# A chunked recurrence whose step matrix becomes block-diagonal over two heads, with the scaled state written by ScalarE

## The chip, the cores and the metric

The kernel runs on one core of one Trainium2 chip. The metric is the device time of one execution in microseconds (us). The core's engines are called as in the profile: PE is TensorE's matmul, PEld its weight load, DVE is VectorE, ACT is ScalarE, POOL is GpSimd, SP is SyncE, which issues most transfers. Each engine works through its own queue in order, and an instruction that waits for a semaphore holds what is behind it.

## The reference

The model is one block of width 1024 over a sequence of 1024: attention with a forget gate (8 heads of 64), an RWKV-7 time mix (8 heads of 64), a gated merge, and a feed-forward part with a convolution. All is in fp32. The change lies in the time mix, whose core is a recurrence over time for each head:

```python
def step(state, inp):
    r_t, w_t, k_t, v_t, a_t, b_t = inp
    sa = jnp.einsum('bhvk,bhk->bhv', state, a_t)
    state = state * w_t[:, :, None, :] + sa[..., None] * b_t[:, :, None, :] + v_t[..., None] * k_t[:, :, None, :]
    y_t = jnp.einsum('bhvk,bhk->bhv', state, r_t)
    return state, y_t
```

## The kernel before

The time mix is computed in chunks of 64 positions, so that only one 64x64 state for each head and chunk is handed on. Two heads sit on the 128 partitions together (head 0 on partitions 0 to 63, head 1 on 64 to 127; HS[h] is the slice). The four head pairs p and two halves hf of the sequence (512 positions, 8 chunks) make eight units. A unit has two generators. `pre` builds its inputs: it loads the decay `cum` and `al` (L707, L709), takes the running sum of cum within each chunk (the scan at L710), its exponentials el and en (L713, L715), the products p (L758), a 31-step triangular inverse on VectorE (L778, L780) with round trips through DRAM (sm, M, se, TT), and the transposes vt and at. `main` first completes the inverse (xi, zi, and the copies of TT at L853), then forms uw (Wt, UV), then mz, from which VectorE writes Zt (L877) and the step matrix Mt (L878: product plus identity, both heads of a chunk stacked as 128x64). The recurrence follows: for each chunk c, sp (which already holds the input part) gets Mt times the state S of that chunk added, one 64x64 product for each head, and S of the next chunk is sp times the chunk's decay pcd (L897, VectorE). At the end all states enter yp with Zt (one 64x64 product for each head and chunk), and the output y is normalised: `head_sums` splits its argument in two parts (L688 on ScalarE, L689 on GpSimd) and sums over each head by two matmuls with blk_r, once for mu and once for va. Then the gate gg is loaded (L929), multiplied in, and the result stored.

A unit has 8 state operations in the first half of the sequence and 7 in the second. The first state of a head pair needs no product, so there are 56 steps with products and 60 state operations. Each product is one `mm`; the profile counts two records for an fp32 product, so 224 in all (L141 is the line of the helper through which nearly all matmuls go).

TensorE's order is written out by the class `Weave`: it keeps a model time, runs the chains `main` and `pre` as they come due, and fills the model time that a `yield` asks for with large matmuls (the projections ps_rkv, qk, v and gt, 128x128 weights by 512 or 256 columns). The recurrence yields 1150 after each step, which puts about six of the 512-wide matmuls, or eleven of the 256-wide ones of v, between two steps. `mm_cost` prices a 64x64 fp32 product at half of what it prices a full-size one of the same output. The other engines' orders come from the tile scheduler, which goes by an estimate of when each input is ready; buffers of the same tag are reused, and a new user waits for the readers of the old one. Zt, Mt and Wt are single buffers, which the split parts of `head_sums` (Zt and Mt) and gg (Wt) take over once the recurrence is through.

What else the change and the prediction touch: L366 (ScalarE's scaled copy of a projection), L272 and L274 (the split of large weights in two parts, on ScalarE and VectorE), L393 (ScalarE's write of q and k), L734 (ScalarE's copy of bk), L805 and L866 (copies of at and uw), L742 (VectorE's ksq). The lines that the changed kernel moves have other numbers there (L853 is L859, L688 is L692).

Of the kernel before, what the change touches and what calls it, by code (L numbers as in the profile page):

```python
# [9 lines left out]
F32 = mybir.dt.float32  # L10
F32R = mybir.dt.float32r
AF = mybir.ActivationFunctionType
ALU = mybir.AluOpType
# [3 lines left out]
S = 1024  # L17
KT = 8
NH = 512
# [3 lines left out]
CH = 64  # L23
NCU = NH // CH
# [13 lines left out]
CST = {}  # L38
# [6 lines left out]
NC1 = 384  # L45
NC2 = CST["blk"][0]
# [86 lines left out]
def hybrid_block(ctx: ExitStack, tc: tile.TileContext, a, out):  # L133
    nc = tc.nc
# [3 lines left out]
    def mm(o, lhsT, rhs, start, stop, more=False):  # L138

        weave.mm_cost(o, lhsT, rhs)  # L140
        nc.tensor.matmul(o, lhsT, rhs, start=start, stop=stop, skip_group_check=more)  # L141
# [5 lines left out]
    def f32(ap):  # L147
        return ap.bitcast(F32)

    tt, stt, ts = nc.vector.tensor_tensor, nc.vector.scalar_tensor_tensor, nc.vector.tensor_scalar  # L150
# [11 lines left out]
    cst = cp.tile([128, NC1], F32R, name="cst")  # L162
# [6 lines left out]

    def C(name):  # L170
        o, k = CST[name]
        return cst[:, o : o + k] if o < NC1 else cst2[:, o - NC1 : o - NC1 + k]

    eye_r, tri_r = C("ident"), C("tri")
    ident, ones = f32(eye_r), f32(C("ones"))
# [68 lines left out]
    marks = {}  # L244
# [101 lines left out]
    with ExitStack() as es:  # L346
        scr = es.enter_context(tc.tile_pool(name="scr", bufs=2, space=bass.MemoryType.DRAM))
        shp = es.enter_context(tc.tile_pool(name="shp", bufs=2))
        cst2 = shp.tile([128, NC2 - NC1], F32, name="cst2", bufs=1)

        def big(name):
            return pb.tile([128, NH], F32, tag="big", name=name)
# [48 lines left out]
        HS = (slice(0, 64), slice(64, 128))  # L401
# [11 lines left out]
        with tc.tile_pool(name="st", bufs=1) as st, tc.tile_pool(name="stp", bufs=2, space=PS) as stp, \  # L413
# [113 lines left out]
                for j in range(2):  # L527
                    nc.sync.dma_start(w2[r * 64 : r * 64 + 64, j * 512 : j * 512 + 512], a["w2a2"][j * 64 : j * 64 + 64, :])
            nc.sync.dma_start(g2, a["g2"])
            nc.sync.dma_start(cst2, a["cst"][:, NC1:NC2])  # L530
            for i in (1, 0):
                for kt in range(KT):
                    mod_add(kt, *m[1 - i])
# [23 lines left out]
        with tc.tile_pool(name="lg", bufs=1, reuse_waits="tile") as lg, \  # L557
# [65 lines left out]
            def forget():  # L623

                wf = lg.tile([128, 8, 40], F32R, tag="wf", name="wf", bufs=1)
                wr = lg.tile([128, 8, 8], F32, tag="wr", name="wr", bufs=1)
                nc.sync.dma_start(wr, a["w_f"])
                ts(wf, cst2[:, 0:320].rearrange("p (k x) -> p k x", x=40), 0.0, None, op0=ALU.mult)
                nc.scalar.copy(wf[:, :, 0:8], wr)
                tt(wf[:, :, 32:40], wr, f32(wf[:, :, 0:8]), op=ALU.subtract)  # L630
                bf = lg.tile([8, 1], F32, tag="bf", name="bf", bufs=1)
                nc.sync.dma_start(bf, a["b_f"])
                prev = None
                for hf in range(2):
                    cs = slice(hf * NH, hf * NH + NH)
                    ps = gen(f"f_{hf}")
                    n = 0
                    for x in u:
                        for kt in range(KT):
                            mm(ps[0:40, :], wf[:, kt, :], x[:, kt, cs], start=n == 0, stop=n == 15)  # L640
# [42 lines left out]
        blk_r = rw.tile([128, 128], F32R, name="blk_r")  # L683
        nc.gpsimd.dma_start(blk_r, a["cst"][:, NC2 : NC2 + 128].bitcast(F32R))

        def head_sums(ps, x, hi, lo):

            nc.scalar.copy(hi, x)  # L688
            nc.gpsimd.tensor_tensor(lo, x, f32(hi), op=ALU.subtract)  # L689
            yield 3400  # L690
            mm(ps, blk_r, hi, start=True, stop=False)
            mm(ps, blk_r, lo, start=False, stop=True)  # L692

        def pre(k, p, hf):
# [5 lines left out]
            def tmp(nm, w=NH, bufs=1, dt=F32):  # L700
                return rw.tile([128, w], dt, tag=nm, name=f"{nm}{n}", bufs=bufs)
# [5 lines left out]
            nc.sync.dma_start(cum, d_lora[0, p, :, cs])  # L707
            al = tmp("al")
            nc.sync.dma_start(al, d_lora[1, p, :, cs])  # L709
            nc.vector.tensor_tensor_scan(cum, C("reset"), cum, initial=0.0, op0=ALU.mult, op1=ALU.add)  # L710
            el = chunk_tile("el", 1, NCU, CH + 1)
            nc.gpsimd.memset(el[:, :, 0:1], 1.0)
            nc.scalar.activation(el[:, :, 1:], c3(cum), AF.Exp, scale=-DEC)  # L713
# [37 lines left out]
            for c0 in range(0, NCU, 4):  # L751
                ps = [gen(f"p1_{n}{h}{c0}") for h in range(2)]
                for c in range(c0, c0 + 4):
                    for h in range(2):
                        mm(ps[h][:, (c - c0) * 128 : (c - c0) * 128 + 128], bk[HS[h], c, BKS[h], :], ar[HS[h], :, c, :],
                           start=True, stop=True)
                for h in range(2):
                    marks["E"] = tt(E[:, c0 : c0 + 4, h, 0:2, :].rearrange("p c a s -> p c (a s)"), hx(ps[h], 128),  # L758
                       C("mask").unsqueeze(1).to_broadcast([128, 4, 128]), op=ALU.mult)
                yield 2200  # L760

            sm = scr.tile([2, NCU, 2, 32, 32], F32, tag="sm", name=f"sm{n}")
# [8 lines left out]
            ready = weave.now + (49500 if k == 0 else 38500)  # L771
            E32 = chunk_tile("E32", 1, 8, 32)
            nc.gpsimd.dma_start(E32, a["cst"][:, CST["einit"][0] :].rearrange("p (j t) -> p j t", t=32))
            t32 = tmp("t32", 256)
            for s in range(31):
                J, W = s // 4 + 1, 31 - s
                tv = t32[:, 0 : J * W].rearrange("p (j w) -> p j w", w=W)
# [46 lines left out]
        def main(k, p, hf):  # L824
# [41 lines left out]
                    nc.scalar.copy(UV[HS[h], c0 : c0 + 4, h, :], pv[HS[h], :, 0, :])  # L866
            yield 2970
            Zt = rw.tile([128, NCU, CH], F32, tag="Zt", name=f"Zt{n}", bufs=1)
            Mt = rw.tile([128, NCU, CH], F32, tag="Mt", name=f"Mt{n}", bufs=1)
            for c0 in range(0, NCU, 4):  # L870
                ps = gen(f"mz{n}{c0}")
                for c in range(c0, c0 + 4):
                    for h in range(2):
                        x = (c - c0) * 128
                        mm(ps[HS[h], x : x + 128], Wt[HS[h], c, :], E[HS[h], c, h, 1:3, :], start=True, stop=True)
                pv = ps.rearrange("p (c a s) -> p c a s", a=2, s=CH)
                tt(Zt[:, c0 : c0 + 4, :], pv[:, :, 0, :], ar[:, 1, c0 : c0 + 4, :], op=ALU.add)  # L877
                tt(Mt[:, c0 : c0 + 4, :], pv[:, :, 1, :], C("i2").unsqueeze(1).to_broadcast([128, 4, CH]), op=ALU.add)  # L878

            yp = py.tile([128, NCU, CH], F32, tag="yp", name=f"yp{n}")  # L880
            sp = py.tile([128, NCU, CH], F32, tag="sp", name=f"sp{n}")
# [9 lines left out]
            last_c = NCU - 1 - hf  # L891
            for c in range(last_c + 1):
                if S[c] is not None:
                    for h in range(2):
                        mm(sp[HS[h], c, :], Mt[HS[h], c, :], S[c][HS[h], :], start=False, stop=c == last_c, more=True)
                S.append(rw.tile([128, CH], F32, tag="state", name=f"S{n}{c}", bufs=9))
                marks["S"] = ts(S[-1], sp[:, c, :], pcd[:, c : c + 1], None, op0=ALU.mult)  # L897
                if c + 1 < NCU:
                    yield 1150

# [10 lines left out]
            def part(nm, i):  # L911
                return rw.tile([128, NH], F32R, tag=nm, name=f"{nm}{i}{n}", bufs=1)

            mu = gen(f"mu{n}")
            yield 700
            yield from head_sums(mu, y, part("Zt", "r"), part("Mt", "r"))
            stt(y, mu, -1.0 / CH, y, op0=ALU.mult, op1=ALU.add)
            ysq = rw.tile([128, NH], F32, tag="ysq", name=f"ysq{n}", bufs=1)
            nc.scalar.activation(ysq, y, AF.Square)
            yield 2700  # L920
            va = gen(f"va{n}")
            yield from head_sums(va, ysq, part("Zt", "s"), part("Mt", "s"))
            rs = rw.tile([128, NH], F32, tag="ysq", name=f"rs{n}", bufs=1)
            nc.scalar.activation(rs, va, AF.Ln, scale=1.0 / CH, bias=epsr[:, 1:2])
            nc.scalar.activation(rs, rs, AF.Exp, scale=-0.5)
            stt(y, y, V("ln_w", p), rs, op0=ALU.mult, op1=ALU.mult)
            stt(y, y, V("ln_b", p), bon, op0=ALU.add, op1=ALU.add)
            gg = rw.tile([128, NH], F32, tag="Wt", name=f"gg{n}", bufs=1)
            nc.sync.dma_start(gg, d_lora[2, p, :, cs])  # L929
            ov = rw.tile([128, NH], F32, tag="ysq", name=f"o{n}", bufs=1)  # L930
            tt(ov, y, gg, op=ALU.mult)
# [1078 lines left out]
```

## Time and profile before

| | us |
|---|---|
| time of 3 runs, median (lowest to highest) | 1674.87 (1674.54 to 1675.46) |
| profiled execution, its own time | 1675.02 |
| its span in the trace | 1673.2 |
| PE busy | 1626.0 (97%) |
| PEld busy | 1341.4 (80%) |
| DVE busy | 1224.8 (73%) |
| ACT busy | 804.6 (48%) |
| POOL busy | 130.5 (8%) |

The span is what the trace covers; the execution's own time has 1.8 us more around it. The busy share is an average over the whole block: the projections, the recurrence (about 250 to 640 us), the attention and the feed-forward part have different limits. In rows of the timeline, the first number is the start in us from the span's start, the second the time from the first start to the last end of the group (matmuls overlap, so the starts tell more than the durations); a bracket tells how long the engine was idle before and what ended that. In rows of groups, the columns are the line, engine, operation, out<-in, shapes and count, then busy us and the mean ns of one, then the idle time before them with what ended it. Rows of waits have the total us, how many, and the longest.

### The profile page before, as it was taken

What the parts mean: (1) busy time and instruction counts of PE and PEld (TensorE: products, weight loads), DVE (VectorE), ACT (ScalarE), POOL (GpSimd) and SP (SyncE); (2) the same over time, 40 slices, a digit from 0 to 9 for tenths busy, and PEclk for the clock granted to TensorE, in tenths of its full rate; (3) what the DMA queues carried; (4) which work ended last, traced back from release to release, by engine and by line L of the source; (5) the groups of instructions that cost most, each with busy time, mean ns of one, the idle gap of its engine ahead of it and who ended that gap; (6) DMA issues with size and microseconds to landing.
All of it is one profiled execution on the core that took longest, in us unless ns stands there. A gap on an engine that the chain in (4) does not pass through costs nothing.

```text
span 1673.2 us, 26130 instructions
## 1 busy us (share of the span) xinstructions
PE 1626.0 (97%) x9806; PEld 1341.4 (80%) x9806; DVE 1224.8 (73%) x2407; ACT 804.6 (48%) x1480; POOL 130.5 (8%) x151
## 2 busy tenths in 40 slices
PE   7999999999999999999999999999999999999998
PEld 7777777787877777888878888888888888888886
DVE  5786777788876625898768546897777777786677
ACT  5563334434344456667632225654444444455455
POOL 0011001101111002221022000000000000000000
PEclk9999989999999999999999999999999999999999
DMA  8487644443342227444087511143322323574463
GB/s 334 146 315 239 181 114 124 130 111 112 102 121 76 90 76 181 131 128 120 34 306 267 213 63 64 63 125 109 107 95 96 119 95 108 192 271 154 129 210 108
DMA packets 121502, 240.77 MB, mean 144 GB/s; under 512 B 40032, under 2 KB 48608, under 8 KB 121376
## 3 DMA queue, kind: packets, MB, share of 16 engines
q1 hardware_dynamic: 112896, 220.74, 40.6%
q0 software_dynamic: 8480, 18.37, 4.2%
q8 instruction: 77, 1.26, 0.3%
q14 instruction: 49, 0.40, 0.1%
HBM read 173.51 MB, written 65.54 MB: 143 GB/s over the span
## 4 chain that ended last, share of the span: by engine, by line
PE 74%; DVE 14%; DMA 6%; ACT 3%; issue 2%; SPq 2%; DVEq 0%; ACTq 0%
PE X L141 14%; PE D L141 13%; PE Y L141 7%; PE wo L141 5%; PE ps_rkv L141 5%; PE br L141 5%; PE gt L141 4%; PE rk_ps L141 3%; PE W L141 3%; PE qk L141 2%; PE lg L141 2%; PE ov L141 2%; PE tp L145 2%; DVE E L780 1%; DVE t L778 1%
## 5 line engine op out<-in xcount | busy, mean ns | idle before, releaser
L141 PE MATMUL D<-op,op 128*128 128x512 f32 x924 | 209.8, 389 | 0.0
L141 PEld LDWEIGHTS D<-op,op 128*128 128x128 f32 x924 | 173.3, 188 | 36.3 <-DVE op L1247 0.3
L141 PE MATMUL X<-T_m,S 128*128 128x512 f32 x440 | 106.9, 389 | 0.0
L141 PEld LDWEIGHTS X<-T_m,S 128*128 128x128 f32 x440 | 82.5, 188 | 17.5 <-ACT x L1537 0.4
L1246 ACT CAST op<-g 128x512 fp32r<-128x512 f32 x77 | 47.8, 621 | 74.8 <-PE D L141 47.8
L1247 DVE TENSOR_TENSOR op<-g,op 128x512 fp32r<-128x512 f32 x77 | 53.1, 689 | 41.5 <-ACT op L1246 41.5
L1497 DVE SCALAR_TENSOR_TENSOR c<-ab,vec,c 128x512 f32<-128x512 f32 x88 | 65.9, 750 | 18.4 <-ACT c L1500 16.8
L778 DVE TENSOR_TENSOR t<-E,M 128x60 f32<-128x60 f32 (+24 forms) x248 | 57.0, 230 | 25.9 <-DMA M<-sm 20.4
L1461 DVE TENSOR_TENSOR A<-ur,A 128x512 fp32r<-128x512 f32 x64 | 44.0, 689 | 39.3 <-ACT A L1457 39.1
L1461 DVE TENSOR_TENSOR S<-ur,S 128x512 fp32r<-128x512 f32 x66 | 45.5, 691 | 34.9 <-ACT S L1457 34.8
L274 DVE TENSOR_TENSOR lo_in<-raw_in,hi_in 128x512 fp32r<-128x512 f32 x84 | 57.6, 726 | 14.0 <-PE gt L141 4.6
L1457 ACT CAST S<-ur 128x512 fp32r<-128x512 f32 x66 | 41.0, 622 | 55.6 <-DVE ur L1450 30.6
L141 PE MATMUL Y<-T_h,S 128*128 128x512 f32 x264 | 65.6, 398 | 1.6 <-ACT T_h L1715 1.0
L272 ACT CAST hi_in<-raw_in 128x1024 fp32r<-128x1024 f32 x42 | 43.8, 1047 | 42.5 <-PE ps_rkv L141 25.0
L141 PE MATMUL Y<-T_h,A 128*128 128x512 f32 x264 | 63.4, 389 | 0.0
L1048 ACT ACTIVATE P<-lg,nm 128x896 f32<-128x896 f32 (+3 forms) x64 | 47.4, 743 | 29.1 <-DVE nm L1044 20.9
L141 PEld LDWEIGHTS Y<-T_h,S 128*128 128x128 f32 x264 | 50.6, 192 | 13.4 <-ACT T_h L1715 1.8
L141 PE MATMUL W<-B_f,A 128*128 128x512 f32 x252 | 60.6, 389 | 0.0
L141 PE MATMUL X<-B_b,A 128*128 128x512 f32 x252 | 60.5, 389 | 0.0
L1457 ACT CAST A<-ur 128x512 fp32r<-128x512 f32 x64 | 39.6, 622 | 43.2 <-PE X L141 33.4
L780 DVE TENSOR_TENSOR E<-E,t 128x60 f32<-128x60 f32 (+24 forms) x248 | 55.2, 223 | 5.7
L141 PEld LDWEIGHTS Y<-T_h,A 128*128 128x128 f32 x264 | 49.5, 188 | 10.3
(480 smaller groups left out, 4125.0 us busy)
## 6 DMA issues: line engine op xcount, KB each, us to landing
raw_in<-in_w_in SPq DMA_DIRECT2D x50, 512.0 KB, 3.8
wm<-in_w_mod SPq DMA_DIRECT2D x48, 512.0 KB, 7.3
ur<-in_w_up SPq DMA_DIRECT2D x44, 512.0 KB, 4.0
g<-d_g SPq DMA_DIRECT2D x35, 512.0 KB, 4.0
d_g<-gs SPq DMA_DIRECT2D x44, 256.0 KB, 2.0
d_g<-c SPq DMA_DIRECT2D x33, 256.0 KB, 4.4
d_st<-qh SPq DMA_DIRECT2D x64, 128.0 KB, 2.4
stA<-d_st POOLq DMA_DIRECT2D x8, 1024.0 KB, 6.6
```

The source lines that it names most:

```text
L141: nc.tensor.matmul(o, lhsT, rhs, start=start, stop=stop, skip_group_check=more)
L145: nc.tensor.transpose(o, i, eye)
L272: nc.scalar.copy(hi, raw)
L274: nc.vector.tensor_tensor(lo[:, c : c + NH], raw[:, c : c + NH], f32(hi[:, c : c + NH]), op=ALU.subtract)
L778: tt(tv, E32[:, 0:J, s : s + 1].to_broadcast([128, J, W]), M32[:, s : s + 1, s + 1 : 32].to_broadcast([128, J, W]), op=ALU.mult)
L780: tt(E32[:, 0:J, s + 1 : 32], E32[:, 0:J, s + 1 : 32], tv, op=ALU.add)
L1048: nc.scalar.activation(e[:, 0:n], lg[:, 0:n], AF.Exp, bias=nm[:, 0:1], accum_out=nm[:, 1:2])
L1246: nc.scalar.copy(hi, src)
L1247: tt(lo, src, f32(hi), op=ALU.subtract)
L1457: nc.scalar.copy(hi, src)
L1461: tt(lo, src, f32(hi), op=ALU.subtract)
L1497: stt(c, ab[:, x + hf * NH : x + hf * NH + NH], V("conv_w", 22 * x + i), c, op0=ALU.mult, op1=ALU.add)
```

## The change

- The step matrix Mt is one persistent tile of 128x128 for each chunk, cleared once by GpSimd. VectorE writes the two 64x64 diagonal blocks of each chunk, one instruction for each head and four chunks (32 in all instead of 16 of both heads), adding the block of `ident`.
- A step is one product of 128x128 weights with the 128x64 state of both heads, instead of two of 64x64.
- The next state is written by ScalarE (activation Copy with the scale taken from pcd) instead of VectorE's tensor_scalar. The number of state buffers goes from 9 to 8.
- To make room: the second constant tile keeps 384 of 704 columns (the mask, and 256 columns of `reset`) and is loaded in two transfers; the scan at L710 runs in two halves of 256 columns; t32 shrinks from 256 to 128 columns; the forget weights are cleared from another tile. Since Mt is no longer a free buffer after the recurrence, the split parts of `head_sums` go to Wt, and gg goes to Zt.

```diff
-        cst2 = shp.tile([128, NC2 - NC1], F32, name="cst2", bufs=1)
+        cst2 = shp.tile([128, 384], F32, name="cst2", bufs=1)
...
-            nc.sync.dma_start(cst2, a["cst"][:, NC1:NC2])
+            for o, c0, w in ((0, CST["mask"][0], 128), (128, CST["reset"][0], 256)):
+                nc.sync.dma_start(cst2[:, o : o + w], a["cst"][:, c0 : c0 + w])
...
+        Mt = rw.tile([128, NCU, 128], F32, name="Mt")
+        nc.gpsimd.memset(Mt, 0.0)
...
-            nc.vector.tensor_tensor_scan(cum, C("reset"), cum, initial=0.0, op0=ALU.mult, op1=ALU.add)
+            for c0 in (0, 256):
+                nc.vector.tensor_tensor_scan(cum[:, c0 : c0 + 256], cst2[:, 128:384], cum[:, c0 : c0 + 256], initial=0.0,
+                                             op0=ALU.mult, op1=ALU.add)
...
-                tt(Mt[:, c0 : c0 + 4, :], pv[:, :, 1, :], C("i2").unsqueeze(1).to_broadcast([128, 4, CH]), op=ALU.add)
+                for h in range(2):
+                    tt(Mt[HS[h], c0 : c0 + 4, HS[h]], pv[HS[h], :, 1, :],
+                       ident[HS[h], HS[h]].unsqueeze(1).to_broadcast([64, 4, CH]), op=ALU.add)
...
-                    for h in range(2):
-                        mm(sp[HS[h], c, :], Mt[HS[h], c, :], S[c][HS[h], :], start=False, stop=c == last_c, more=True)
-                S.append(rw.tile([128, CH], F32, tag="state", name=f"S{n}{c}", bufs=9))
-                marks["S"] = ts(S[-1], sp[:, c, :], pcd[:, c : c + 1], None, op0=ALU.mult)
+                    mm(sp[:, c, :], Mt[:, c, :], S[c], start=False, stop=c == last_c, more=True)
+                S.append(rw.tile([128, CH], F32, tag="state", name=f"S{n}{c}", bufs=8))
+                marks["S"] = nc.scalar.activation(S[-1], sp[:, c, :], AF.Copy, scale=pcd[:, c : c + 1])
...
-            yield from head_sums(mu, y, part("Zt", "r"), part("Mt", "r"))
+            yield from head_sums(mu, y, part("Zt", "r"), part("Wt", "r"))
...
-            gg = rw.tile([128, NH], F32, tag="Wt", name=f"gg{n}", bufs=1)
+            gg = rw.tile([128, NH], F32, tag="Zt", name=f"gg{n}", bufs=1)
```

More of the change, by code (lines that the diff above doesn't have):

```diff
@@ L171, in C @@
         o, k = CST[name]
-        return cst[:, o : o + k] if o < NC1 else cst2[:, o - NC1 : o - NC1 + k]
+        return cst[:, o : o + k]
     eye_r, tri_r = C("ident"), C("tri")
@@ L627, in forget @@
                 nc.sync.dma_start(wr, a["w_f"])
-                ts(wf, cst2[:, 0:320].rearrange("p (k x) -> p k x", x=40), 0.0, None, op0=ALU.mult)
+                ts(wf, f32(cst[:, 0:320]).rearrange("p (k x) -> p k x", x=40), 0.0, None, op0=ALU.mult)
                 nc.scalar.copy(wf[:, :, 0:8], wr)
@@ L758, in pre @@
                     marks["E"] = tt(E[:, c0 : c0 + 4, h, 0:2, :].rearrange("p c a s -> p c (a s)"), hx(ps[h], 128),
-                       C("mask").unsqueeze(1).to_broadcast([128, 4, 128]), op=ALU.mult)
+                       cst2[:, 0:128].unsqueeze(1).to_broadcast([128, 4, 128]), op=ALU.mult)
                 yield 2200
@@ L773, in pre @@
             nc.gpsimd.dma_start(E32, a["cst"][:, CST["einit"][0] :].rearrange("p (j t) -> p j t", t=32))
-            t32 = tmp("t32", 256)
+            t32 = tmp("t32", 128)
             for s in range(31):
@@ L868, in main @@
             Zt = rw.tile([128, NCU, CH], F32, tag="Zt", name=f"Zt{n}", bufs=1)
-            Mt = rw.tile([128, NCU, CH], F32, tag="Mt", name=f"Mt{n}", bufs=1)
             for c0 in range(0, NCU, 4):
@@ L921, in main @@
             va = gen(f"va{n}")
-            yield from head_sums(va, ysq, part("Zt", "s"), part("Mt", "s"))
+            yield from head_sums(va, ysq, part("Zt", "s"), part("Wt", "s"))
             rs = rw.tile([128, NH], F32, tag="ysq", name=f"rs{n}", bufs=1)
```

## The prediction

> **What bounds the kernel now.** I read the page's first and fourth parts, then the busy time by stage, then the waits of TensorE in the stage that the change touches, then its groups of instructions and the timeline around a few steps. The page's head, busy line and chain:
>
> ```profile
> span 1673.2 us, 26130 instructions
> PE 1626.0 (97%) x9806; PEld 1341.4 (80%) x9806; DVE 1224.8 (73%) x2407; ACT 804.6 (48%) x1480; POOL 130.5 (8%) x151
> PE 74%; DVE 14%; DMA 6%; ACT 3%; issue 2%; SPq 2%; DVEq 0%; ACTq 0%
> ```
>
> TensorE is busy for 97% of the span and holds 74% of the chain. The recurrence lies between 250 and 640 us; its row gives the stretch, its length, then PE, PEld, DVE, ACT, POOL, the granted clock, the DMA share and GB/s:
>
> ```profile
> 250.00:640.00 390.00, 380.46 (x3642) 306.12 (x3641) 269.71 (x762) 175.65 (x312) 53.89 (x65) 1.00 0.38 109
> ```
>
> PE is busy 380.46 of 390.00 us, at full clock; VectorE has 269.71 (69%), ScalarE 175.65 (45%). Only 9.54 us are PE's idle time. Three of its waits, from 240 to 640 us (total, times, longest), and the two groups that the change replaces:
>
> ```profile
> PE sp L141 <- DVE S L897: 4.0, 7, 1.3
> PE q L141 <- DVE QA L805: 2.0, 2, 1.7
> PE uw L141 <- ACT TT L853: 1.9, 1, 1.9
> ```
> ```profile
> L141 PE MATMUL sp<-S,Mt 64*64 64x64 f32 x224 | 18.6, 242 | 4.1 <-DVE S L897 4.0
> L897 DVE TENSOR_SCALAR S<-sp,pcd 128x64 f32<-128x64 f32 x60 | 16.8, 281 | 26.0 <-PE sp L141 25.8
> ```
>
> The reader should see two things. The recurrence is a serial chain (product, scaled state, next product), but it is not the bound: six large matmuls are placed between two steps, and the state is late only 7 times, for 4.0 us. What counts is the time that a step takes away from TensorE, and what arrives late because of the new engine. The 224 records are 56 steps of four (two heads, two passes each).
>
> **The step on TensorE.** A step among 512-wide and one among 256-wide filler:
>
> ```profile
> 259.10 0.33 PE L141 MATMUL sp<-S,Mt 64*64 64x64 f32 x4
> 259.36 0.73 PE L141 MATMUL ps_rkv<-u_lo,hi_in 128*128 128x512 f32 x2
> 259.48 0.28 DVE L897 TENSOR_SCALAR S<-sp,pcd 128x64 f32<-128x64 f32 x1 [1.35 <-PE sp L141]
> 259.93 1.09 PE L141 MATMUL ps_rkv<-u_hi,lo_in 128*128 128x512 f32 x4
> 260.13 1.05 ACT L272 CAST hi_in<-raw_in 128x1024 fp32r<-128x1024 f32 x1 [3.00 <-PE ps_rkv L141]
> 260.95 0.33 PE L141 MATMUL sp<-S,Mt 64*64 64x64 f32 x4
> ```
> ```profile
> 358.32 0.33 PE L141 MATMUL sp<-S,Mt 64*64 64x64 f32 x4
> 358.58 1.10 PE L141 MATMUL v<-lo_v,u_hi 128*128 128x256 f32 x7
> 359.52 0.64 PE L141 MATMUL v<-hi_v,u_hi 128*128 128x256 f32 x4
> 360.09 0.33 PE L141 MATMUL sp<-S,Mt 64*64 64x64 f32 x4
> ```
>
> The trace of before has no full-size step, but it has full-size 128-column records set among the same matmuls, the transposes:
>
> ```profile
> 268.22 1.76 PE L141 MATMUL qk<-u_lo,hi_in 128*128 128x512 f32 x7
> 269.82 0.27 PE L145 MATMUL vt<-cst,v 128*128 128x128 f32 x1
> ...
> 270.58 0.27 PE L145 MATMUL at<-cst,ar 128*128 128x128 f32 x1
> 270.61 0.48 PE L141 MATMUL qk<-u_lo,hi_in 128*128 128x512 f32 x1
> 270.93 0.39 PE L141 MATMUL mu<-Ztr,blk_r 128*128 128x512 f32 x1
> ```
>
> Seven large matmuls take 268.22 to 269.82, 0.229 us each. From one step to the next, 259.10 to 260.95, are 1.85 us for six of them, so the old step takes 1.85 - 6 x 0.229 = 0.48. Among 256-wide ones (about 0.12 each by the four from 359.52 on, less the drain at their end) it takes 1.77 - 11 x 0.12 = 0.45. The eight transposes, one record each, start 0.76/7 = 0.109 apart; 268.22 to 270.93 is 2.71 us for them and eight large matmuls, so they add 2.71 - 8 x 0.229 = 0.88. Two records instead of eight: 0.88 - 6 x 0.109 = 0.23. A new step is two full-size records, and I take 0.23. It saves 0.25 among the wide matmuls and 0.22 among the narrow ones.
>
> Of 56 steps, four (the last of each first-half unit) run straight into the 64x64 yp products: the change of tile is then paid there instead, and I count them at nothing. Some 38 of the others lie among wide filler and 14 among narrow: 38 x 0.25 + 14 x 0.22 = 12.6, say 12.5 us. The bounds: a step can't cost less than its two records as such, 0.109 + 0.03 to the next matmul (270.58 to 270.61), so 0.14 and 17 us saved. At the worst the 0.10 or so of entering stays (the old step's excess is not the tile's) and the second weight load isn't hidden (0.109 instead of 0.03): 0.41, and 3 us saved. I take 12.5, since the transposes are the same shape in the same surroundings. All of it lies on the path, PE's order being fixed and full.
>
> **The state on ScalarE.** The nearest rows for its price:
>
> ```profile
> L366 ACT ACTIVATE sh_rkv<-ps_rkv,vec 128x512 f32<-128x512 f32 x24 | 16.5, 690 | 20.7 <-PE ps_rkv L141 20.5
> L393 ACT ACTIVATE qh<-qk 128x512 fp32r<-128x512 f32 x16 | 9.5, 594 | 10.0 <-DVE gb L242 3.2 <-DVE t L778 2.6 <-DMA d_st<-qh 2.1
> L866 ACT COPY UV<-uw 64x256 f32<-64x256 f32 x32 | 11.7, 366 | 13.4 <-DVE Wt L864 12.8
> ```
>
> The scale from a pointer adds 690 - 594 = 96 ns; a column costs (594 - 366)/256 = 0.89 ns; so 64 columns with a pointer take 366 - 192 x 0.89 + 96 = 291 ns, between 0.20 (the pointer free) and 0.37 (no cheaper than 256 columns). VectorE's was 281: alone, nothing. ScalarE gains 60 x 0.29 = 17 us of work and VectorE loses 16.8. The chain: S started 0.38 after its product (259.10, 259.48) and ended at 0.66; the new step period is 1.85 - 0.25 = 1.60, so 0.9 us are spare. One op of ScalarE ahead of S is thus covered unless it is a full cast (1.05) that starts just before it.
> The Trainium skill speaks against this move: "ScalarE: Activation LUTs", Rules for kernel authors, sends multiplications to VectorE, and What ACT_TABLE_LOAD costs prices the op at 186 + 93 + 0.833 x 64 = 332 ns, an estimate by that page; exposed in full, 56 x 0.05 would put the sum 2.9 us higher. It is weighed as rival (4).
>
> What counts is ScalarE's queue, which is in order. In the new order most S stand behind casts and activations whose inputs are ready in time. One is not: in unit 1 (second half of head pair 0) the second S stands behind the copy at L688, which waits for VectorE's ksq:
>
> ```profile
> 303.87 0.75 DVE L742 SCALAR_TENSOR_TENSOR ksq<-r,vec,al 128x512 f32<-128x512 f32 x1
> 304.65 0.62 ACT L688 CAST cum<-ksq 128x512 fp32r<-128x512 f32 x1 [0.88 <-DVE ksq L742]
> 304.98 0.33 PE L141 MATMUL sp<-S,Mt 64*64 64x64 f32 x4 [0.27 <-DVE S L897]
> 307.19 0.33 PE L141 MATMUL sp<-S,Mt 64*64 64x64 f32 x4 [0.30 <-DVE S L897]
> ```
>
> ksq ends at 304.62, some 0.7 later with the added Mt work below; then 0.5 of copy and 0.29 of S: the next product starts near 306.2 where 304.45 would do, a stall of 1.75. The seven waits of now (4.0) had S behind VectorE's long operations and go with it. Net: 1.75 - 4.0 = -2.25, between -4 (no stall) and +4 (three more units like this one).
>
> **Mt in two parts, the scan, the loads.**
>
> ```profile
> L878 DVE TENSOR_TENSOR Mt<-mz,cst 128x256 f32<-128x256 f32 x16 | 6.7, 416 | 0.0
> L805 DVE COPY QA<-at 64x256 f32<-64x256 f32 x32 | 13.5, 422 | 7.1 <-PE at L145 6.6
> L710 DVE TENSOR_TENSOR_SCAN cum<-cst,cum 128x512 f32<-128x512 f32 x8 | 9.8, 1222 | 7.7 <-DMA cum<-d_lora 7.7
> ```
>
> Half the partitions cost the same (422 against 416), so 16 more instructions add 16 x 0.42 = 6.7 us; the scan in two halves adds a start each, between nothing and a whole 64-column operation (281 ns); I take 0.1 x 8. VectorE's balance is -16.8 + 6.7 + 0.8 = -9 us. The added 0.84 a unit lies between the mz products and the first step, with the sp and yp products of the inputs in between, and is hidden. The memset of Mt is once on GpSimd, early. The constants come in two transfers instead of one, far ahead of their use: nothing.
>
> gg now takes Zt's place, which va's product reads, and SP's order puts it next to the load of cum in most units; SP is in order, so cum waits for va too. Two places bear on it:
>
> ```profile
> 287.89 0.63 ACT L713 ACTIVATE el<-cum 128x512 f32<-128x512 f32 x1 [4.12 <-DVE cum L710]
> 288.94 0.73 ACT L853 COPY TT<-zi 32x256 f32<-32x256 f32 x2
> ```
> ```profile
> 380.28 0.39 PE L141 MATMUL va<-Mts,blk_r 128*128 128x512 f32 x1
> 380.97 0.34 SPq L707 DMA_DIRECT2D cum<-d_lora  x1
> ```
>
> In unit 1 the TT copies stood behind el, which waited 4.12 for cum's scan: that is the 1.9 wait of uw. In the new order they stand ahead of it, and the wait goes. In three later units el stays ahead, and gg's issue (0.33 to 0.37 of queue, and a share of the transfer) delays cum by 0.3 to 1: I take 0.9 in all. Net -1, between -2 and +2.
>
> **The sum.** The profiled run took 1675.02, span 1673.2, and stands 0.15 above the median shown. A faster PE comes sooner to its other waits. Producers lead by more than a unit's gain of 1.6 us in the tightest case I found:
>
> ```profile
> 426.10 0.89 DVE L836 STREAM_TRANSPOSE X<-TT 32x256 f32<-32x256 f32 x2
> 431.80 0.38 PE L141 MATMUL xi<-X,E 32*32 32x32 f32 x12
> ```
>
> (4.8 us), but q's wait on QA, 2.0, has no lead and may double: +2. So 1675.02 - 12.5 - 2.25 - 1 + 2 = 1661.3; against the median 1661.
>
> **The rivals.** (1) A full-size step costs its upper bound, 0.41: the tile shape is not what the old step paid for, and the change does not do what it says on TensorE. For it: these are fp32 products with two weight loads and a data wait, not transposes. Against: entering a transpose group costs nothing visible. 1675.02 - 3 - 1.25 = 1671.
> (2) On the other side: ScalarE's queue becomes the bound. If in each of the eight units two steps stall as in unit 1 (behind L688's or L734's copies, which wait for VectorE, or behind casts), 16 x 1.75 = 28: 1675.02 - 12.5 - 4.0 - 1 + 2 + 28 = 1687.5. It decides from 15.5 us of stalls on, 0.28 a step. For it: the in-order queue, and casts as long as the spare time. Against: VectorE did this between more work (69% busy) and lost 4.0.
> (3) No difference: PE's gain is handed over to waits on VectorE, whose 31-step loop (L778, L780) and DMA round trips stand on the chain, and to cum's later load. That takes some 12.5 us of new idle time: about 1674. Against it, the lead of 4.8 us and VectorE's 9 us less.
> (4) The state costs more on ScalarE, and every step shows it: at 0.37 against 0.28, 56 x 0.09 = 5 us, 1666. That needs the 0.9 us of spare time to be gone in every step, which no row suggests. The Trainium skill's rule on multiplications, above, points this way.
>
> **Chances.** Forecast 0.63, (1) 0.10, (2) 0.12, (3) 0.10, (4) 0.05. The measurement tells about 0.2%, 3.3 us, from no change. Faster 0.78, same 0.10, slower 0.12. The range goes from 1653 (17 saved on the steps, 4 on the state's waits, 2 at uw, and q's wait 1 longer) to 1676, where no change and a little of (3)'s spread end; above it lies (2).
>
> **What would show it.** The group sp<-S,Mt with 128*128 tiles, 112 records, and a step period of about 1.60 among wide matmuls (1.85 now): right if within 1.55 to 1.70, wrong at 1.78. S on ScalarE at 0.29 (0.20 to 0.37). Waits of sp on ScalarE's S of about 1.8 us in all, in unit 1 near 300 us; several units with over 1 us would be rival (2). uw's wait of 1.9 gone. VectorE down by about 9 us, ScalarE up by 17. The stretch of the recurrence shorter by 13 us, with PE still over 97% busy; if PE's busy share falls there with the period right, it is (3).

## The result, and the profile after

The changed kernel takes 1664.32 us (median of 4 runs, 1660.79 to 1667.48) against 1674.70 (1674.46 to 1675.46): ratio 0.9938, 95% interval 0.9914 to 0.9962. Measured again in a second group (below) it took 1661.47 against 1674.88, ratio 0.9922 (0.9902 to 0.9942). The forecast was 1661, faster. The profiled execution took 1660.79, so the trace shows 14.2 us of gain where the medians of the two groups show 10.4 and 13.4; a part of the 14.2 is the clock, not the change (below).

The page of the changed kernel, its head, busy line and chain:

```profile
span 1659.0 us, 25949 instructions
PE 1613.1 (97%) x9694; PEld 1343.8 (81%) x9694; DVE 1223.7 (74%) x2371; ACT 822.6 (50%) x1540; POOL 128.9 (8%) x152
PE 61%; DVE 4%; DMA 1%; ACT 1%; issue 1%; SPq 0%; DVEq 0%; ACTq 0%
```

PE's busy time is 12.9 us shorter, and ScalarE's 18.0 longer (60 states). The groups that the change touches, after:

```profile
L141 PE MATMUL sp<-S,Mt 128*128 128x64 f32 x112 | 19.0, 251 | 2.3 <-ACT S L903 2.3
L903 ACT ACTIVATE S<-sp,pcd 128x64 f32<-128x64 f32 x60 | 18.7, 312 | 41.3 <-PE sp L141 41.1
L884 DVE TENSOR_TENSOR Mt<-mz,cst 64x256 f32<-64x256 f32 x32 | 13.3, 416 | 0.3
```

The busy sum of the group sp<-S,Mt did not fall (18.6 before, 19.0 now). The records of a step overlap (before, four of 242 ns took 0.33 us together), so their durations don't add up to what a step takes from TensorE. The gain is in the starts, and the timeline shows it:

```profile
249.56 0.33 PE L141 MATMUL sp<-S,Mt 128*128 128x64 f32 x2
249.69 1.18 PE L141 MATMUL ps_rkv<-u_hi,lo_in 128*128 128x512 f32 x4
250.71 0.62 PE L141 MATMUL ps_rkv<-u_hi,hi_in 128*128 128x512 f32 x2
251.17 0.33 PE L141 MATMUL sp<-S,Mt 128*128 128x64 f32 x2
```

From step to step are 1.61 us with the same six large matmuls between, where it was 1.85. This holds throughout: of the steps with six such matmuls behind them and no wait, all 27 of before take 1.85 or 1.86, and 27 of the 29 now take 1.60 to 1.62. TensorE's waits from 240 to 660 us (total, times, longest):

```profile
PE rk_ps L141 <- DVE gs L340: 3.4, 1, 3.4
PE sp L141 <- ACT S L903: 2.3, 2, 1.5
PE v L141 <- DVE vs L956: 1.7, 3, 1.0
PE rk_ps L141 <- ACT gm L1164: 1.4, 2, 1.2
PE va L141 <- POOL Wts L693: 0.9, 1, 0.9
PE uw L141 <- ACT TT L859: 0.7, 1, 0.7
```

The state's waits fell from 4.0 to 2.3, uw's from 1.9 to 0.7, and q's 2.0 is gone. At the top stands one that the kernel before did not have: rk_ps, the first product of the next stage, waits 3.4 us. Its place, in rows of the timeline:

```profile
608.33 1.00 POOL L998 DMA_DIRECT2D stB<-d_st  x1
610.44 0.39 PE L141 MATMUL va<-Wts,blk_r 128*128 128x512 f32 x1
610.67 0.32 SPq L935 DMA_DIRECT2D gg<-d_lora  x1
618.24 0.70 POOL L996 DMA_DIRECT2D stA<-d_st  x1
621.05 0.69 DVE L937 TENSOR_TENSOR o<-y,gg 128x512 f32<-128x512 f32 x1 [7.23 <-DMA gg<-d_lora]
621.66 0.68 DVE L340 SCALAR_TENSOR_TENSOR gs<-gt,gs 128x512 f32<-128x512 f32 x1
622.39 2.92 PE L141 MATMUL rk_ps<-u_hi,hi_in 128*128 128x512 f32 x8 [3.39 <-DVE gs L340]
```

The gg of the last unit is issued as soon as va's product has read Zt's buffer. By then GpSimd's loads for the attention (stA, stB) are under way, and gg lands 10.3 us later, where the median of the eight is 3.4. VectorE sits idle for it, with the gate's product (L340) queued behind o, and TensorE waits for that. Before the change the last gg was issued at 598.8, ahead of those loads. The end of the stage is measured from the last gt, the last large matmul of the gate's projection, to the first lg, a product of the attention. The rows, first of before, then of after (a row of eight matmuls starts its last one 0.39 us, the duration of one, before its end):

```profile
636.00 1.98 PE L141 MATMUL gt<-u_hi,lo_in 128*128 128x512 f32 x8
649.41 0.39 PE L141 MATMUL lg<-stA 128*128 128x512 f32 x1
```
```profile
617.03 1.98 PE L141 MATMUL gt<-u_hi,lo_in 128*128 128x512 f32 x8
635.37 0.39 PE L141 MATMUL lg<-stA 128*128 128x512 f32 x1
```

The sequence took 11.8 us before (637.59 to 649.41) and 16.8 now (618.61 to 635.37). So the changed kernel was 19.0 us ahead at the last gt and gave 4.9 back.

Not all of the 19.0 is the change. The granted clock, the number behind the five busy times (third from the right, 1.00 at full speed), was lower in the profiled run of before, ahead of the first recurrence (the first row is of before, the second of after):

```profile
224.00:236.00 12.00, 10.83 (x86) 8.11 (x86) 9.71 (x36) 4.51 (x8) 0.19 (x1) 0.57 0.50 130
```
```profile
224.00:236.00 12.00, 11.34 (x110) 8.73 (x112) 10.88 (x40) 5.84 (x11) 0.19 (x1) 0.86 0.54 134
```

The first uw, which no step precedes, started at 238.54 before and 235.19 after:

```profile
238.54 1.96 PE L141 MATMUL uw<-QA,TT 64*64 64x128 f32 x32
```
```profile
235.19 1.96 PE L141 MATMUL uw<-QA,TT 64*64 64x128 f32 x32
```

So 3.3 us came ahead of all that the change does on TensorE. They are not the change's: e9 (below), which is the kernel before up to there, started its first uw at 234.88, with 0.89 granted from 220 to 236 us where before had 0.68. By the two rows of windows above, the clock would account for 12 x (0.86 - 0.57) = 3.5 us, an estimate.

What the recurrence itself gained is read from the first step to the last (each row, of before and of after, gives the durations of one record, then the starts of the group's first and last one):

```profile
L141 PE MATMUL sp<-S,Mt x224: 218/242/267, 253.0 to 615.8; 64*64 64x64 f32 x112
```
```profile
L141 PE MATMUL sp<-S,Mt x112: 217/273/323, 249.6 to 595.8; 128*128 128x64 f32 x112
```

That stretch fell from 362.8 to 346.2 us, by 16.6, of which 13.5 are PE's busy time (353.3 to 339.7) and 3.1 its idle time.

### The profile page after: what moved, and what is told of

Same layout as the page of the kernel before. It is cut to its first block, busy times and chain, and to the rows that moved or that the text cites. A ratio compares the mean times of both kernels' runs of the same rounds, so it can differ in the third digit from the quotient of the medians.

```text
span 1659.0 us, 25949 instructions
## 1 busy us (share of the span) xinstructions
PE 1613.1 (97%) x9694; PEld 1343.8 (81%) x9694; DVE 1223.7 (74%) x2371; ACT 822.6 (50%) x1540; POOL 128.9 (8%) x152
## 4 chain that ended last, share of the span: by engine, by line
PE 61%; DVE 4%; DMA 1%; ACT 1%; issue 1%; SPq 0%; DVEq 0%; ACTq 0%
PE X L141 14%; PE D L141 13%; PE Y L141 7%; PE wo L141 5%; PE br L141 5%; PE rk_ps L141 4%; PE gt L141 3%; PE W L141 3%; PE lg L141 2%; PE ov L141 2%; PE tp L145 2%; DMA gg<-d_lora 1%; DVE nm L1050 1%; DVE P L1060 1%; DMA g<-d_gate 0%
## 5 line engine op out<-in xcount | busy, mean ns | idle before, releaser
L141 PEld LDWEIGHTS X<-T_m,S 128*128 128x128 f32 x440 | 82.5, 188 | 17.6 <-ACT x L1543 0.4
L141 PEld LDWEIGHTS Y<-T_h,S 128*128 128x128 f32 x264 | 50.6, 192 | 13.4 <-ACT T_h L1721 1.7
L141 PEld LDWEIGHTS Y<-T_h,A 128*128 128x128 f32 x264 | 49.5, 188 | 10.3
```

## The experiments

The theory was that of the prediction, with what the first profile added: the product gives some 12.5 us, the state's move a net 1.7 by the waits, and the late gg costs 4 to 5. The rivals: it is the state's move that gives the gain, and the spread between runs lies in the recurrence. The experiments came in three groups: e1 to e4 undo one part of the change at a time, e5 to e8 test what these showed, e9 to e12 complete the comparisons. Medians of one group's kernels stand against the same runs of the kernel before, whose median was 1674.88, 1674.79 and 1674.61 in the three groups.

**e1, the changed kernel again.** No edit.

> The changed kernel once more, unaltered, as the reference of this group and for the spread of its runs (1660.79 to 1667.48 so far, before 1674.46 to 1675.46). My theory: the recurrence gains the same as in the first profile, 19 to 20 us up to the last large matmul of the gate projection less what the clock gave, and 4 to 5 us are lost again behind it, where the last gg comes late; the spread comes from that late load and from the clock near 224 to 236 us (0.57 granted in the profile of before, 0.86 after), so the profile shows 1661 to 1668 with the differences at these two places. Rival: the spread lies inside the recurrence (waits of the state on ScalarE), and the two places look as in the first profile.

1661.47 us (1659.29 to 1664.54). The profile has the wait of rk_ps on gs L340 again (2.7 us), 16.0 us from the last gt to the first lg, and 17.7 gained at the last gt. The granted clock from 220 to 236 us was 1.00 in this run, and the stretch from the first step to the last 347.5 us (346.2 in the first profile). The pattern repeats, and these two executions do not differ much in the recurrence; the slowest ones (up to 1667.48) were not traced, so where their time goes is not shown. Medians of this kernel differ by 2.9 us between the groups, so smaller differences of medians are not read below.

**e2, the product alone.**

```diff
-                marks["S"] = nc.scalar.activation(S[-1], sp[:, c, :], AF.Copy, scale=pcd[:, c : c + 1])
+                marks["S"] = ts(S[-1], sp[:, c, :], pcd[:, c : c + 1], None, op0=ALU.mult)
```

> The changed kernel with the state written by VectorE again; product, Mt and buffers as changed. My theory (the product gives nearly all, 12.5 us; the state's move a net 1.7 by the waits, 4.0 before against 2.3 after): 1664 to 1667, waits of sp on VectorE's S of 2 to 5 us. Rival (the gain comes from taking S out of VectorE's queue): 1670 or more.

**e3, the state's move alone.**

```diff
-                    mm(sp[:, c, :], Mt[:, c, :], S[c], start=False, stop=c == last_c, more=True)
+                    for h in range(2):
+                        mm(sp[HS[h], c, :], Mt[HS[h], c, HS[h]], S[c][HS[h], :], start=False, stop=c == last_c, more=True)
```

> The changed kernel with two 64x64 products a step again; the state stays on ScalarE, Mt and buffers as changed. My theory: step period 1.85 us, the 12.5 us are gone: 1675 to 1679, waits of the state on ScalarE 2 to 3 us with unit 1's 1.7 among them. Rival (the move of S gives the gain): 1668 or less.

**e4, neither: the layout alone.** Both edits together.

> Neither: two 64x64 products a step and the state on VectorE, with Mt in two blocks, the split scan, gg in Zt's place and the other buffers as changed. My theory: the layout alone costs the late gg at the end, 4 to 5 us, less 1 to 3 us at other waits (uw, q): 1674.7 + 2 to 4 = 1676 to 1679. Rival (the layout costs nothing, the late gg is due to the shorter recurrence alone): 1674 to 1675.

| | product | state on | us (lowest to highest) | ratio to before (95%) |
|---|---|---|---|---|
| e1 | one full-size | ScalarE | 1661.47 (1659.29 to 1664.54) | 0.9922 (0.9902 to 0.9942) |
| e2 | one full-size | VectorE | 1678.93 (1674.37 to 1681.61) | 1.0029 (1.0014 to 1.0044) |
| e3 | two 64x64 | ScalarE | 1687.82 (1682.08 to 1692.00) | 1.0076 (1.0046 to 1.0106) |
| e4 | two 64x64 | VectorE | 1696.63 (1695.56 to 1698.24) | 1.0131 (1.0110 to 1.0153) |

e2, e3 and e4 came out above what my theory expected; e2 lies where the rival put it. Neither half is faster than the kernel before, and what I had called layout costs 22 us by itself. Waits of TensorE, of e4:

```profile
PE rk_ps L141 <- DVE gs L340: 12.3, 1, 12.3
PE sp L141 <- DVE S L904: 10.7, 9, 1.9
```

and of e3:

```profile
PE rk_ps L141 <- DVE gs L340: 11.8, 1, 11.8
PE sp L141 <- ACT S L904: 1.2, 2, 0.7
```

Two costs show. With the state on VectorE it is late 10.7 us in all (4.0 before the change; 11.7 in e2), with the state on ScalarE it isn't (1.2). And the late gg costs more than in the changed kernel: 12 us. A new theory: the layout's 22 us are the late gg and something that delays VectorE ahead of the steps, where the two-part write of Mt is the work that was added. The second group takes each away.

**e5, gg early.** The last unit's gg goes to kr's buffer, which nobody uses by then.

```diff
-            gg = rw.tile([128, NH], F32, tag="Zt", name=f"gg{n}", bufs=1)
+            gg = rw.tile([128, NH], F32, tag="Zt" if k < 7 else "kr", name=f"gg{n}", bufs=1)
```

> The changed kernel, with the gate gg of the last unit alone in the buffer of kr, which is free by then, so that its load is issued long before the last va product instead of behind it. My theory (the late gg, in a burst of loads for the attention, holds VectorE's o, the gate's last product on VectorE and so the first rk_ps for 3.4 us, and the clock is low right after): the wait of rk_ps on gs L340 falls from 3.4 to under 0.5, the time from the last gt to the first lg from 16.8 to 11.8 us (11.8 before the change), the whole by 4 to 5 us to about 1657 to 1659. Rival (the loads for the attention or the store of the gate set the end of this stage, gg only stands in their way): under 1 us, 1661 to 1664.

1657.62 us (1655.96 to 1659.00), ratio 0.9901 (0.9886 to 0.9916). gg is issued at 563.4; the timeline of the place now:

```profile
617.59 1.98 PE L141 MATMUL gt<-u_hi,lo_in 128*128 128x512 f32 x8
619.40 1.98 PE L141 MATMUL rk_ps<-u_hi,hi_in 128*128 128x512 f32 x8
...
630.62 0.39 PE L141 MATMUL lg<-stA 128*128 128x512 f32 x1
```

rk_ps follows gt without a wait, and 11.5 us lie between the last gt (619.17) and lg. The loads for the attention do not set the end of this stage; gg did.

**e7, the layout with gg early.** e4 with e5's edit.

> Two products a step and the state on VectorE as in e4, with the last gg loaded early. My theory: of e4's 22 us over the kernel before, 12 to 14 stand between the last gt and the first lg and go, the 7 us of the recurrence stay: 1681 to 1684. Rival (the loss sits in the order of the other loads): 1690 or more.

1685.54 us (1682.56 to 1691.41): 11.1 below e4. The wait of rk_ps on gs is gone, the state's waits are 11.0. That is 1.5 above the expected range, and the median lies below the rival's 1690.

**e8, the layout with Mt written in one part.**

```diff
-                for h in range(2):
-                    tt(Mt[HS[h], c0 : c0 + 4, HS[h]], pv[HS[h], :, 1, :],
-                       ident[HS[h], HS[h]].unsqueeze(1).to_broadcast([64, 4, CH]), op=ALU.add)
+                tt(Mt[:, c0 : c0 + 4, :], pv[:, :, 1, :], cst2[:, 384:448].unsqueeze(1).to_broadcast([128, 4, CH]), op=ALU.add)
```

(Mt has 64 columns a chunk here, and the second constant tile 64 more, for the stacked identity.)

> e4 with Mt written as before by one instruction of 128 partitions for four chunks (64 columns a chunk, the stacked identity kept in the second constant tile), all else as e4. It tells where the waits of the state on VectorE come from: 4.0 us before, 10.7 in e4. If the two-part write of Mt, 0.84 us a unit ahead of the steps in VectorE's queue, delays the chain that S stands in: waits of sp on S fall to 4 to 6 us and the last gt comes 5 us earlier than in e4, the whole at 1689 to 1692. If they come from the order around it (the split scan, gg's place): 9 to 11 us of waits, 1695 to 1698.

1686.10 us (1683.53 to 1690.89), 10.5 below e4, more than expected. The wait, in the same view:

```profile
PE sp L141 <- DVE S L902: 3.2, 7, 0.9
```

The two-part write makes the state late on VectorE. The two costs account for e4: 1696.63 - 11.1 - 10.5 = 1675.0, the kernel before. No run takes both away, and the medians leave some 4 us of room, but the stretch from the first step to the last says the same of the recurrence: 372.6 us in e4, 362.3 in e8, 362.8 in the kernel before. What else belongs to the layout (the split scan, the constants, the smaller buffers) costs nothing there that can be seen.

**e9, the two-part write in the kernel before.**

```diff
-                tt(Mt[:, c0 : c0 + 4, :], pv[:, :, 1, :], C("i2").unsqueeze(1).to_broadcast([128, 4, CH]), op=ALU.add)
+                for h in range(2):
+                    tt(Mt[HS[h], c0 : c0 + 4, :], pv[HS[h], :, 1, :],
+                       C("i2")[HS[h], :].unsqueeze(1).to_broadcast([64, 4, CH]), op=ALU.add)
```

> The kernel before, with nothing changed but the write of Mt: two instructions of 64 partitions for each four chunks instead of one of 128, into the same 64 columns. My theory, from e4 and e8: the 0.84 us more a unit on VectorE ahead of the steps makes the state late there: waits of sp on S grow from 4.0 to 8 to 11 us, the whole by 4 to 8 us to 1679 to 1683. Rival (it takes the other changes of the layout as well): waits of 4 to 5 us and 1675 to 1676.

```profile
PE sp L141 <- DVE S L899: 10.7, 9, 2.1
```

1686.45 us (1682.92 to 1688.90), ratio 1.0065 (1.0041 to 1.0089). Sixteen more instructions of 0.42 us, 6.7 us of VectorE's time in a kernel where VectorE is busy for 73%, cost 11.8. The waits of the state come from them alone; they are as many as in e4, and the same in sum. The stretch from the first step to the last is 374.7 us against 362.8, 11.9 longer: 6.7 are the state's waits, 1.6 those of q (3.6 against 2.0), and some 1.7 a low granted clock from 514 to 518 us, right behind a wait of 2.14 us for the state. The time is above the expected range, on the theory's side.

**e10 and e11, the two halves with gg early.** e2 and e3 with e5's edit.

> The changed kernel with the state on VectorE and the last gg loaded early (e2 with e5's edit), the third corner beside e5 (1657.6) and e7 (1685.5). My theory: waits of sp on S 11 to 12 us; 1672 to 1676, that is 10 to 13 us below e7 by the product alone.

> The changed kernel with two products a step and the last gg loaded early (e3 with e5's edit), the fourth corner. My theory: waits of sp on S 1 to 3 us; 1670 to 1674: 9 to 12 us below e7 by the state's move, 12 to 14 above e5 by the product. Together with e5, e7 and e10: the two effects add up, each 9 to 14 us once the late gg is out of the way.

1674.75 us (1670.60 to 1678.03; ratio 1.0001, 0.9989 to 1.0014) and 1672.64 (1668.94 to 1676.36; 0.9983, 0.9969 to 0.9997), with waits of the state of 12.0 and 1.2 us. Both times lie in their expected ranges. With e5 and e7 that gives, gg being out of the way: the product is worth 10.8 us with the state on VectorE (e7 to e10) and 15.0 with it on ScalarE (e11 to e5); the state's move 12.9 (e7 to e11) and 17.1 (e10 to e5). The upper values are above the 9 to 14 expected. But by the intervals of the ratios each of these differences is uncertain by some 3 to 5 us, so the medians alone can't tell whether the effects add or differ by 4 us. The traces can. The table has the stretch from the first step to the last, and what a low granted clock took of it (the sum over windows of 2 us of length times one minus the clock):

| | product | state on | first to last step, us | low clock, us | without it |
|---|---|---|---|---|---|
| e7 | two 64x64 | VectorE | 372.2 | 1.7 | 370.5 |
| e10 | one full-size | VectorE | 362.7 | 5.1 | 357.6 |
| e11 | two 64x64 | ScalarE | 359.1 | 0 | 359.1 |
| e5 | one full-size | ScalarE | 346.2 | 0 | 346.2 |
| before | two 64x64 | VectorE | 362.8 | 1.7 | 361.1 |

Without the low clock the product is worth 12.9 us with either engine and the state's move 11.4 with either product: the two add, and neither gain is the other's. The clock of e10 is low right behind its long waits for the state, here the one of 2.65 us:

```profile
303.98 0.43 PE L141 MATMUL sp<-S,Mt 128*128 128x64 f32 x2 [2.65 <-DVE S L903]
```
```profile
304.00:308.00 4.00, 3.17 (x11) 2.21 (x12) 3.72 (x9) 0.14 (x1) 1.45 (x1) 0.64 0.63 197
308.00:312.00 4.00, 4.00 (x11) 3.17 (x11) 1.73 (x10) 1.04 (x1) 0.00 (x0) 0.50 0.75 197
```

These are single traces, but kernels with the same recurrence agree: 372.6 in e4 and 372.2 in e7, 358.4 in e3 and 359.1 in e11, 346.2 and 347.5 in the changed kernel.

**e6, bk's copy off ScalarE.** The 1.5 us wait of the changed kernel, in unit 1, in rows of its timeline:

```profile
296.50 0.62 ACT L740 COPY bk<-bk 64x512 f32<-64x512 f32 x1 [7.48 <-DVE bk L739]
297.15 1.05 ACT L272 CAST hi_in<-raw_in 128x1024 fp32r<-128x1024 f32 x1
298.10 0.31 ACT L903 ACTIVATE S<-sp,pcd 128x64 f32<-128x64 f32 x1
298.46 0.43 PE L141 MATMUL sp<-S,Mt 128*128 128x64 f32 x2 [1.49 <-ACT S L903]
```

S stands behind a cast, and the cast behind a copy that waited for VectorE.

```diff
-            nc.scalar.copy(bk[64:128, :, 2, :], bk[64:128, :, 0, :])
+            nc.gpsimd.tensor_copy(bk[64:128, :, 2, :], bk[64:128, :, 0, :])
```

> The changed kernel with the copy of bk (L740) on GpSimd instead of ScalarE, so that in unit 1 no S stands behind a copy that waits for VectorE. My theory: the wait of 1.5 us at 298 us goes, sp's waits on ScalarE's S fall from 2.3 to about 0.9, the whole by 1 to 1.5 us (1660 to 1663). Rival (what stands behind bk's copy, the cast of 1.05 us, is enough): the wait stays at 1 us or more.

1665.27 us (1661.50 to 1670.35): no gain. Its trace shows why:

```profile
302.90 0.62 ACT L692 CAST cum<-ksq 128x512 fp32r<-128x512 f32 x1 [2.82 <-DVE ksq L748]
303.42 0.31 ACT L903 ACTIVATE S<-sp,pcd 128x64 f32<-128x64 f32 x1
303.79 0.43 PE L141 MATMUL sp<-S,Mt 128*128 128x64 f32 x2 [1.80 <-ACT S L903]
```

The wait went one copy further, to the one that the prediction had named (L688 there, L692 here), at the 1.8 it had priced. Both expectations missed it.

**e12, both copies off ScalarE, gg early.** The edits of e5 and e6, and the first part of the bonus sums on VectorE (`head_sums` takes the copying operation as an argument; of the edit only its use is shown):

```diff
-            yield from head_sums(bp, rkb, tmp("cum", dt=F32R), tmp("en", dt=F32R))
+            yield from head_sums(bp, rkb, tmp("cum", dt=F32R), tmp("en", dt=F32R), nc.vector.tensor_copy)
```

> e5 with both copies that hold S in unit 1 taken off ScalarE: bk's (L740) on GpSimd, and the first part of the bonus sums (ksq to cum, L692) on VectorE. My theory: the wait of 1.5 us near 298 us goes and does not come back one step later as in e6 (1.87 us there, behind the cum copy), the one near 543 us (behind the gate's L341) stays: waits of sp on S about 1 us, 1656 to 1657. Rival (VectorE, with the copy, hands the delay to its own products): waits of 2 us or more elsewhere, 1657 to 1660.

1661.26 us (1659.77 to 1662.33), 3.6 above e5 and just above the rival's range. The state's waits fell to 1.3, near the 1 expected, and unit 1's is gone; but the whole is slower, as the rival had it:

```profile
PE v L141 <- DVE vs L956: 3.3, 2, 2.4
```

v's wait on VectorE grew from 1.8 in e5 to 3.3. Most of the rest is again the clock: right behind the longest of these waits (2.4 us, ending at 447.3) the granted clock was low, which took 1.7 us.

```profile
446.00:450.00 4.00, 2.69 (x12) 2.69 (x13) 3.93 (x12) 0.25 (x1) 0.84 (x1) 0.62 0.33 81
```

The stretch from the first step to the last is 3.3 longer than in e5 (349.5 against 346.2), which is these 1.7 and 1.2 more of waits in all, but for 0.4. In e6 the clock fell in the same way, behind the wait of 1.80 shown above. e5 is the fastest version run: 1657.62, 17.2 us below the kernel before.

## Why the prediction was right, point by point

The forecast was 1661, and the two medians were 1664.32 and 1661.47. The cost of the step, the largest term, was right in its mechanism and its size; that the rest of the sum came out is in good part luck, since several wrong terms cancel.

- **The step on TensorE** (0.23 from the transposes, 12.5 us saved): right, for the reason given. 1.61 - 6 x 0.229 = 0.24, the period lies within 1.55 to 1.70, and the product is worth 12.9 in the traces (10.8 to 15.0 by the medians). Rival (1), the upper bound, is refuted by the period.
- **The state on ScalarE** (291 ns, 0.20 to 0.37): 312. The estimate of 332 by the Trainium skill ("ScalarE: Activation LUTs", What ACT_TABLE_LOAD costs) lies 20 above the trace. The slower operation was not exposed in every step: the period is 1.60 to 1.62 with no wait, and with the state on ScalarE its waits were 1.2 to 3.5 in all kernels run, against 10.7 to 12.0 on VectorE beside the same write of Mt. So rival (4) is refuted. The Trainium skill's rule that multiplications belong on VectorE ("ScalarE: Activation LUTs", Rules for kernel authors) goes by the speed per element. Here the engine with the slower operation (312 ns against 281) was worth 11.4 us in the traces (12.9 to 17.1 by the medians), since it came to the state sooner (the waits above).
- **The queue in unit 1** (a stall of 1.75): right in the unit and the size (1.49), wrong by one step and one copy: the first S, behind bk's copy (named under rival (2) only) and a cast. The second wait, 0.83 at 542.9 behind the gate's L341, was not foreseen. In sum 2.3, not 1.75. Rival (2), such stalls in every unit, is refuted.
- **Mt in two parts** ("hidden", nothing): this step was wrong in its reason, and only came out because another part covered it. I named the products between mz and the first step as cover. They cover the write itself, not the queue: VectorE then runs late into the steps, and a state standing in its queue waits 10.7 us (e4, e9). The price of one instruction was right (416 ns, as forecast), its effect was not: 370.5 - 361.1 = 9.4 us of the stretch where the state stays on VectorE (e7 against before). The cover was the state's move to ScalarE. I had read that move as worth the 4.0 us of waits in the trace of before, less the stall in unit 1, 2.25 in all; in the company of the two-part write it is worth 11.4. The two errors, 9.4 and 9.2, are the same waits and cancel: that this part of the sum came out is luck. What the move is worth without the two-part write was not run.
- **gg in Zt's place** (0.9 us at cum): the step that failed. I looked at the loads of gg that stand beside a load of cum, and not at the last, which has no unit after it but the attention's loads beside it. It cost 4.9 us in the trace, 3.4 of them the wait and the rest about the low clock behind it (1.7), and 3.9 to 6.7 by the medians (e5 against e1 and against the first result).
- **uw** (1.9 gone, 0.9 back): 1.9 to 0.7, right in sum. **q** (+2): wrong in sign. Its wait is absent in all runs with one product a step (the changed kernel, e1, e2, e5, e6, e10 and e12), and 2.4 to 3.6 in e3, e4, e7, e8, e9 and e11: it goes with two products a step. Why was not tested.
- **The sum:** the 14.2 us between the two profiles are 3.4 ahead of the first step (the clock), 16.6 from the first step to the last, -1.0 from there to the last gt (va's 0.9) and -4.9 for gg: 14.1. Of the 16.6, 3.1 are idle time (the state's 1.7, q's 2.0 and uw's 1.2, less v's 1.0 and smaller ones), 1.7 a low clock that only before has there (476 to 481 us, behind q's wait), and 11.8 are left for the 56 steps. So the forecast of 1661 stands by two pairs of errors that nearly cancel: 4.9 for gg not counted against 4.0 for q of the wrong sign (2.0 gained, 2.0 charged), and the write of Mt against the state's move, above.
- **The signs that were named:** 112 records, the period, S's duration and ScalarE (18.0 up for 17) came as said; uw's wait fell to 0.7 instead of going. The stretch of the recurrence got 16.6 us shorter for 13, with PE busy for 98% of it, so rival (3), new idle time, is refuted.
- **VectorE** (down 9): not as forecast on the page, whose busy time fell by 1.1 only. The sums of its groups do fall by 8.7 (S -16.8, Mt +6.6 among them). Records overlap, and the page counts a moment once; I draw nothing from it.

## What to carry to other kernels

When a full engine order has a small matmul in it, price it by the distance between the starts of its neighbours, not by its duration; the duration hardly changed here (242 to 251 ns) while what the step took halved (0.48 to 0.24 us). A part that adds little busy time can cost more than that when it stands in a queue that a serial chain goes through: 6.7 us of writes cost 11.8. Moving the chain to another engine, or taking the added work out of its queue, is then worth far more than the waits in the old trace say. When a buffer changes hands, follow each of its users to the last one: the instance at the end of a stage meets other neighbours than those in its middle. And when an experiment gives more or less than its waits, read the granted clock right behind them.

## What the runs showed of the hardware that I had not expected

- After the 3.4 us in which TensorE waited for the late gg, the granted clock was 0.68 from 622 to 626 us and 0.89 from 626 to 630; eight matmuls of rk_ps took 2.92 us where they take 1.98 at full clock. The wait thus cost more than its length; in e5, without it, they took 1.98.
- Shorter waits did the same in the recurrence. In before the clock fell behind q's wait of 1.72 us (0.60 from 476 to 480), in e10 behind two of 2.65 us for the state, in e12 behind v's 2.40. Summed over windows of 2 us, each such fall took 1.7 us or twice that. That the wait brings the low clock is read from the order of the two alone. Not every wait of this length has one: e8 and e11 had none behind q's 2.30 and 2.40. After the wait for gg, eight matmuls took 3.54 us in e6 and 2.12 in e2, with 2.5 us of wait in both. What decides it was not tested.
- One 256 KB load took 10.3 us among the attention's loads, against 2.5 to 3.7 before the change. It was the same with one product a step in e1, e2 and e6 (9.3 to 9.5, and 2.5 to 2.7 us of wait). With two, in e3, e4 and e8, VectorE's product that needs it started 17.6 to 18.2 us behind its issue, and rk_ps waited 11.8 to 12.3. In these three the gate's store is issued right ahead of gg and the attention's second burst of loads 6.4 us behind it; in the others the store comes right behind gg, and the burst 7.6 us after. Which of the two makes the difference is open: no run isolated it.
